# Attention weights times values in bursts of eight tiles, with the row sums behind them, and a smaller pool for weight operands

## Chip, cores and metric

The kernel runs on one core of one Trainium2 chip. The metric is the device time of one execution in microseconds (us), as the median of several runs. TensorE is called PE below, VectorE DVE, ScalarE ACT, GpSimd POOL and SyncE SP; PEld is PE's weight load, which runs beside its matmuls.

## What is computed

One layer of an encoder over 2048 tokens of width 1024, in float32. Cut to its core, the reference reads:

```python
def reference(x, ...):
    q_a, k_a, v_a, f_a, q_b, k_b, v_b = jnp.split(x @ w_in, SPLITS, axis=-1)
    y_a = forgetting_attention(q_a, k_a, v_a, log_sigmoid(f_a + b_forget))  # 8 heads, causal, FoX
    y_b = chunked_band_attention(q_b, k_b, v_b, rel_bias)                   # 8 heads, own chunk of 64 and 8 before
    x = layer_norm(ALPHA * x + concat(y_a, y_b) @ w_out)
    u = causal_conv(x @ w_up)                                               # width 3, 5632 columns
    value, gate = jnp.split(u, 2, axis=-1)
    return layer_norm(ALPHA * x + (value * gelu(gate)) @ w_down)
# in both attentions: out = softmax(q k^T / 8 + bias) v, per head of 64 columns
```

## The kernel before

Products that need float32 accuracy are made from operands split into a high and a low part (type float32r): `mm3` (lines 182 to 186) issues three matmuls, high by high, high by low and low by high. The split itself (`split`, lines 174 to 180) is one ACT copy (line 177), which makes the high part, and one DVE subtraction (line 180), which makes the low part. All of PE's big products run through `mm3`: the projections of the tokens, the output product, and both products of the feed-forward part.

**Order of the work.** The projections (`projection`) are a dense stream that is advanced a few matmuls at a time by `weave`, while `attention` (from line 498) yields once per tile of 128 keys. The attention runs twice over the heads: once with query chunks 0 and 1 (512 queries each), once with chunks 2 and 3. One unit is a head and a query chunk: 4 to 16 tiles of keys in the forgetting heads (pairs p below 4, called FoX), 4 or 8 in the band heads. What PE executes in the end is an order that a scheduler made when the program was built; it may pull instructions of one stage between those of another, and each engine runs its own list strictly in order.

**One tile.** `logits` (from line 594) makes the scores of 128 keys by up to 512 queries in a PSUM tile `st` (lines 611 and 612, two matmuls; the pool has TB = 2 buffers), adds a bias on DVE where the tile needs one (618, 621), and ACT writes the exponentials to a tile `pt` (line 623; PT = 10 buffers). `total` (629 to 632) adds each `pt` on POOL to a running tile `sums` (NSUM = 3 buffers).

**Value products.** GROUP = 4 tiles `pt` are collected; LAG_P = 4 tiles later `weigh` (693 to 698) multiplies each by its value tile `vv` into the PSUM tile `y`. A value tile has 64 columns, half of PE's array; tiles alternate between the two halves of `y`, `half = HD * (n % 2)`. These are plain float32 products, and each stands in the trace as two matmul records, while each float32r product is one.

**Row sums.** After a unit's last tile `close` joins the two halves of `y`. After the second head of a pair it defers `finish` by another LAG_S = 4 tiles. `finish` (646 to 659) sums `sums` over the 128 partitions with a product by ones (line 650, 64 columns again, one for each of the pair's heads), ACT copies the result to `row` (652; 2 buffers), DVE takes reciprocals and multiplies `yt` (656 to 658), and a DMA stores `y_d`.

**Scores' maxima.** `maxima` (from line 545) runs one unit ahead: products at line 574, maxima on DVE (577, 582). At its start SP loads `qa` and `qb` (lines 552 to 554).

**Operands for later stages.** `prepare_weights` (from line 271) is a generator, advanced once every PRE = 9 yields of the projections from yield PRE0 = 60 on. It makes 16 operands from `w_out` and 77 from `w_down` (11 blocks of 7; 55 of the 77 are a sum or difference of two tiles). It loads four raw tiles of 256 KB (`w_raw`, line 288), yields, then makes one operand per step: a DVE sum or difference (279), the split into the two halves of the one buffer `w_hl`, and one store of 512 KB (282). All DMAs are issued by SP, in order, a DMA waiting there for its buffer and its data.

Of the kernel before, what the change touches and what calls it, by code (L numbers as in the profile page):

```python
# [10 lines left out]
F32 = mybir.dt.float32  # L11
# [8 lines left out]
P = 128  # L20
# [15 lines left out]
SCALE = HD ** -0.5  # L36
NEG = -1e30
LOWEST = -3e38
PT = 10
GROUP = 4  # L40
RATE1, RATE2 = 1.1, 0.6
KV, NKB, NSUM = 5, 7, 3
DLY_E = 10
VAT = (1, 0)
VPOS = (1, 0)
WFREE = 8
LAG_P = 4
HP = 1
LAG_S = 4
LAG_R = 2  # L50
UNIT = 1.0
UNITB = 1.4
# [27 lines left out]
    ((7,), (), ((0, 1), (1, 1))),  # L80
)

PRE0, PRE = 60, 9
AHEAD_L, AHEAD_P, RESERVE = 5, 2, 16
DLY_V, DLY_R, DLY_Z = 32, 16, 16
WNEXT = 3
# [13 lines left out]
def f32(ap):  # L100
    return ap.bitcast(F32)
# [3 lines left out]
def hymba_layer(  # L105
# [165 lines left out]
    def prepare_weights(pool):  # L271

        def parts(dst, u, v=None, op=None):
            hl = tl(pool, [P, 2, CH], F32R, "w_hl")
            if v is not None:
                src = f32(hl[:, 1])
                nc.vector.tensor_tensor(src, u, v, op=op)
                u = src  # L280
            split(hl[:, 0], hl[:, 1], u, nc.scalar, nc.vector)
            nc.sync.dma_start(dst.rearrange("l p m -> p l m"), f32(hl))

        def load(src, tiles):
            raws = []
            for n, (i, j) in enumerate(tiles):
                raws.append(tl(pool, [P, CH], F32, f"w_raw{n}"))
                nc.sync.dma_start(raws[n], src[i * P : i * P + P, CH * j : CH * j + CH])
            return raws

        for k in range(0, KT, 2):
            tiles = [(k + n // 2, n % 2) for n in range(4)]
            raws = load(w_out, tiles)
            yield
            for raw, (i, j) in zip(raws, tiles):
                yield
                parts(wo_d[i, j], raw)
        HF = NF // 2
        for k in range(HF):
            raws = load(w_down, [(HF * i + k, j) for i in range(2) for j in range(2)])  # L300
            yield
            for n in DOWN:
                yield
                (k0, l0), v, op = DOWN[n][3:6]
                parts(wd_d[k, n], raws[2 * k0 + l0], v and raws[2 * v[0] + v[1]], op)


    def projection(mem, banks, state):
# [188 lines left out]
    def attention(pools, chunks, ready):  # L497
# [148 lines left out]
        def finish(p, c, sums, yt):  # L646

            ss = tl(ps_s, [P, CH], F32, "sc")
            for s in range(2):
                nc.tensor.matmul(ss[HD * s : HD * s + HD], ones, sums[s], start=True, stop=True)  # L650
            rs = tl(yp, [P, CH], F32, "row", 2)
            nc.scalar.activation(rs, ss, AF.Copy)

            def divide(t):
                part = rs[:, t * P : t * P + P]
                nc.vector.reciprocal(part, part)
                if t == TQ - 1:
                    nc.vector.tensor_mul(yt, rs, yt)
                    nc.sync.dma_start(y_d[p, :, c * CH : (c + 1) * CH], yt)

            for t in range(TQ):
                defer(LAG_R + t, lambda t=t: divide(t))
# [37 lines left out]
        def close(p, s, c, y, acc):  # L700
            if s == 0:
                yts[p, c] = tl(yp, [P, CH], F32, "yt", 3)
                sums[p, c] = acc
            join(s, c, y, yts[p, c])
            if s == 1:
                defer(LAG_S, lambda: finish(p, c, (sums[p, c], acc), yts[p, c]))

        hd, qs, ahead = start(0)
        run_all(ahead)
        for i, (p, s, c) in enumerate(work):  # L710
            nhd, nqs, ahead = start(i + 1)
            if p < 4 or c == 0:
                order = list(range(TQ * c + TQ))
            else:
                order = [TQ * c - 1, TQ * c] + list(range(TQ * c - 4, TQ * c - 1)) + list(range(TQ * c + 1, TQ * c + TQ))
            acc = tl(yp, [P, CH], F32, "sums", NSUM)
            y = tl(ps_y, [P, CH], F32, "y")
            pieces = 0
            if i + 1 < len(work):
                c1 = work[i + 1][2]  # L720
                pieces = TQ * (c1 + 1 if work[i + 1][0] < 4 else min(2, c1 + 1))
            done = 0
            tiles = []
            for n, j in enumerate(order):
                run_later(now)
                tiles.append(logits(p, s, c, hd, qs, j))
                if n:
                    total(acc, tiles[0][1] if n == 1 else None, *tiles[-1][1:])
                last = n == len(order) - 1
                if len(tiles) == GROUP:  # L730
                    defer(LAG_P, lambda y=y, t=tiles, n=n, last=last: weigh(y, t, n < GROUP, last))
                    tiles = []
                if last:
                    defer(LAG_P, lambda p=p, s=s, c=c, y=y, acc=acc: close(p, s, c, y, acc))
                while done < pieces and done * len(order) < FRAC * pieces * (n + 1):
                    next(ahead, None)
                    done += 1
                now += 1
                yield (UNIT if p < 4 else UNITB) * (UC0 if c == 0 else 1.0)
            run_all(ahead)  # L740
            hd, qs = nhd, nqs
# [652 lines left out]
```

## Time and profile before

| what | before |
|---|---|
| median of the runs | 2792.08 us (lowest 2785.5) |
| the profiled execution's own time | 2789.79 us |
| its span, first to last instruction | 2788.0 us |
| granted PE clock, mean over the span | 0.993 |
| busy: PE, DVE, ACT, POOL | 98%, 70%, 42%, 22% |

The span is what the profiler saw; 1.8 us lie around it. Busy time of PE is the time in which a matmul record is open. Matmuls overlap in the pipeline, so the cost of one is read from the distance between starts, not from its own length. Idle time before a row stands in square brackets with what ended it.

### The profile page before, as it was taken

The numbers are of one execution on the slowest core, as the hardware profiler recorded it, in microseconds if no ns is written. First come the engines' busy times: TensorE is split into PE (matmuls) and PEld (weight loads), VectorE is DVE, ScalarE is ACT, GpSimd is POOL, SyncE is SP. The second block draws the span as 40 slices with busy tenths as digits, with TensorE's granted clock in tenths as the row PEclk, the third lists the DMA queues.
The fourth block names the chain that finished last, engine by engine and source line by source line (L and its number), as shares of the span: only waits on it lengthen the run. The fifth ranks groups of instructions, "written<-read, shape, count | busy, mean of one in ns | idle before, by whom it ended". The sixth has DMA issues, their size and how long they took to land.

```text
span 2788.0 us, 38642 instructions
## 1 busy us (share of the span) xinstructions
PE 2724.5 (98%) x12632; PEld 2045.3 (73%) x12632; DVE 1941.7 (70%) x3577; ACT 1160.7 (42%) x2004; POOL 623.2 (22%) x754
## 2 busy tenths in 40 slices
PE   9999999999999999999998999999999999999998
PEld 7676767675666656766786888888887788888886
DVE  4557576777677655668568888876568877777559
ACT  4434444444444443433225555553222555544221
POOL 2235242327567555333000000000000000000000
PEclk9999999999999999999999999999999999999999
DMA  8666767665455444677894444428778222236974
GB/s 242 197 207 196 228 194 229 211 201 169 144 182 182 137 144 153 199 198 217 293 328 142 141 166 156 155 83 311 260 247 322 87 80 81 78 88 206 323 227 161
DMA packets 324618, 527.40 MB, mean 189 GB/s; under 512 B 70688, under 2 KB 86176, under 8 KB 324416
## 3 DMA queue, kind: packets, MB, share of 16 engines
q1 hardware_dynamic: 324416, 524.93, 59.1%
q8 instruction: 100, 1.64, 0.2%
q14 instruction: 102, 0.84, 0.1%
HBM read 362.65 MB, written 162.14 MB: 188 GB/s over the span
## 4 chain that ended last, share of the span: by engine, by line
PE 84%; DVE 4%; DMA 4%; ACT 1%; issue 1%; POOL 0%; SPq 0%; DVEq 0%; ACTq 0%; POOLq 0%
PE acc L184 21%; PE acc L186 21%; PE acc L185 21%; PE y L698 8%; PE st L611 4%; PE sc L574 4%; PE st L612 3%; DMA qb<-qh_d 1%; PE sc L650 1%; DVE slot L180 1%; DVE slot L1132 1%; DMA slot<-in_w_v_dram 1%; DMA wd_d<-w_hl 1%; PE acc L841 0%; DVE slot L816 0%
## 5 line engine op out<-in xcount | busy, mean ns | idle before, releaser
L184 PE MATMUL acc<-slot,slot 128*128 128x512 f32 (+2 forms) x3064 | 1165.7, 381 | 17.9 <-ACT slot L177 17.9
L186 PE MATMUL acc<-slot,slot 128*128 128x512 f32 (+2 forms) x3064 | 1160.5, 379 | 6.6 <-DVE slot L180 6.6
L185 PE MATMUL acc<-slot,slot 128*128 128x512 f32 (+2 forms) x3064 | 1161.3, 379 | 0.0
L177 ACT ACTIVATE slot<-slot 128x512 fp32r<-128x512 f32 (+1 forms) x680 | 416.4, 626 | 674.2 <-DVE slot L1121 193.0
L184 PEld LDWEIGHTS acc<-slot,slot 128*128 128x128 f32 x3064 | 580.4, 189 | 135.9 <-ACT slot L177 23.5
L186 PEld LDWEIGHTS acc<-slot,slot 128*128 128x128 f32 x3064 | 579.7, 189 | 126.2 <-DVE slot L180 10.8
L185 PEld LDWEIGHTS acc<-slot,slot 128*128 128x128 f32 x3064 | 580.4, 189 | 112.6 <-issue 2.8
L180 DVE TENSOR_TENSOR slot<-slot,slot 128x512 fp32r<-128x512 f32 (+1 forms) x652 | 450.7, 707 | 194.4 <-ACT slot L177 167.9
L632 POOL TENSOR_TENSOR sums<-sums,pt 128x512 f32<-128x512 f32 (+3 forms) x416 | 426.0, 1024 | 251.9 <-ACT pt L623 189.0
L623 ACT ACTIVATE pt<-st 128x512 f32<-128x512 f32 (+3 forms) x544 | 261.7, 492 | 333.4 <-PE st L612 121.4
L698 PE MATMUL y<-pt,vv 128*64 128x512 f32 (+3 forms) x1088 | 281.6, 505 | 0.2 <-DVE yt L640 0.2
L611 PE MATMUL st<-qa,ka 128*128 128x512 f32 (+2 forms) x544 | 209.0, 385 | 9.0 <-ACT pt L623 8.5
L574 PE MATMUL sc<-kb,qb 66*128 66x512 f32 (+2 forms) x544 | 186.6, 373 | 10.8 <-DMA qb<-qh_d 8.1
L612 PE MATMUL st<-qb,kb 97*128 97x512 f32 (+2 forms) x544 | 189.9, 357 | 4.4 <-ACT qb L592 3.9
L577 DVE TENSOR_REDUCE mx<-sc 128x1 f32<-128x512 f32 x192 | 127.9, 686 | 80.0 <-PE sc L574 78.3
L611 PEld LDWEIGHTS st<-qa,ka 128*128 128x128 f32 x544 | 103.0, 189 | 96.0 <-issue 44.1
L698 PEld LDWEIGHTS y<-pt,vv 128*64 128x64 f32 x1088 | 82.0, 136 | 124.2 <-issue 111.5
L574 PEld LDWEIGHTS sc<-kb,qb 66*128 66x128 f32 x544 | 99.5, 190 | 78.6 <-DVE mx L582 17.5
L856 DVE SCALAR_TENSOR_TENSOR v<-u,cw,v 128x1024 f32<-128x1024 f32 x88 | 113.0, 1285 | 62.4 <-ACT v L855 44.2
L1005 POOL COPY u<-halo 128x2 f32<-128x2 f32 x44 | 17.6, 401 | 620.8 <-DVE v L857 620.8
L582 DVE CUSTOM_DVE_ANT_0 junk<-sc,bq 128x512 bf16<-128x512 f32 (+2 forms) x224 | 108.2, 483 | 49.4 <-PE sc L574 40.2
L632 POOL TENSOR_TENSOR sums<-pt 128x384 f32<-128x384 f32 (+1 forms) x64 | 79.5, 1243 | 255.4 <-PE sc L650 181.4
(116 smaller groups left out, 2250.3 us busy)
## 6 DMA issues: line engine op xcount, KB each, us to landing
slot<-wd_d SPq DMA_DIRECT2D x308, 256.0 KB
slot<-in_w_up_dram SPq DMA_DIRECT2D x176, 256.0 KB
wd_d<-w_hl SPq DMA_DIRECT2D x77, 512.0 KB
slot<-wo_d SPq DMA_DIRECT2D x128, 256.0 KB
h_d<-v SPq DMA_DIRECT2D x44, 512.0 KB
slot<-h_d SPq DMA_DIRECT2D x88, 256.0 KB
slot<-in_w_qk_dram SPq DMA_DIRECT2D x66, 256.0 KB
xq_d<-slot SPq DMA_DIRECT2D x56, 256.0 KB
```

The costliest lines, as they stand in the source:

```text
L177: nc.scalar.activation(hi, src, AF.Copy)
L180: lo_eng.tensor_tensor(lo, src, f32(hi), op=ALU.subtract)
L184: nc.tensor.matmul(acc, wh, mh, start=first, stop=False, **more)
L185: nc.tensor.matmul(acc, wh, ml, start=False, stop=False, **more)
L186: nc.tensor.matmul(acc, wl, mh, start=False, stop=last, **more)
L574: nc.tensor.matmul(sc[:, m0:m1], qb[:KR, tq], kb[:KR, m0:m1], start=True, stop=True)
L577: nc.vector.tensor_reduce(m, sc[:, k0:k1], axis=AX.X, op=ALU.max)
L611: nc.tensor.matmul(st[:, w2], ka[:, js], qa[:, w2], start=True, stop=False)
L612: nc.tensor.matmul(st[:, w2], kb[:KM, js], qb[:KM, w2], start=False, stop=True)
L623: nc.scalar.activation(pt[:, w], st[:, w], AF.Exp)
L632: nc.gpsimd.tensor_tensor(acc[:, w], (acc if first is None else first)[:, w], pt[:, w], op=ALU.add)
L698: nc.tensor.matmul(y[half, w], v, pt[:, w], start=first and n < 2, stop=last and n >= len(tiles) - 2)
```

## The change

Eight tiles are collected instead of four, with LAG_P = 3; a unit's remaining tiles are taken with its last tile, so that units of 4 and 12 tiles end in a burst of four. `finish` is no longer deferred by LAG_S but called by `close` at once. There are 13 buffers `pt` instead of 10 and one buffer `row` instead of two. `prepare_weights` loads its operands one by one, a second tile `w_v` where a sum or difference is made, combines and splits in place, and stores the two parts with two DMAs of 256 KB; its pool is `w_lo` twice, `w_hi` and `w_v`. It has two steps to an operand and is advanced every PRE = 5 yields. Line numbers after it are lower by 1 to 5: line 698 becomes 693, 650 becomes 645, 623 becomes 618, 177 becomes 176.

```diff
-PT = 10
-GROUP = 4
+PT = 13
+GROUP = 8
-LAG_P = 4
+LAG_P = 3
-LAG_S = 4
-PRE0, PRE = 60, 9
+PRE0, PRE = 60, 5
...
-        def parts(dst, u, v=None, op=None):
-            hl = tl(pool, [P, 2, CH], F32R, "w_hl")
+        def rows(src, i, j):
+            return src[i * P : i * P + P, CH * j : CH * j + CH]
+
+        def operand(dst, u, v=None, op=None):
+            lo, hi = tl(pool, [P, CH], F32, "w_lo", 2), tl(pool, [P, CH], F32R, "w_hi")
+            nc.sync.dma_start(lo, u)
             if v is not None:
-                src = f32(hl[:, 1])
-                nc.vector.tensor_tensor(src, u, v, op=op)
-                u = src
-            split(hl[:, 0], hl[:, 1], u, nc.scalar, nc.vector)
-            nc.sync.dma_start(dst.rearrange("l p m -> p l m"), f32(hl))
...
+                tmp = tl(pool, [P, CH], F32, "w_v")
+                nc.sync.dma_start(tmp, v)
             yield
+            if v is not None:
+                nc.vector.tensor_tensor(lo, lo, tmp, op=op)
+            split(hi, lo, lo, nc.scalar, nc.vector)
+            nc.sync.dma_start(dst[0], f32(hi))
+            nc.sync.dma_start(dst[1], lo)
+            yield
...
-            rs = tl(yp, [P, CH], F32, "row", 2)
+            rs = tl(yp, [P, CH], F32, "row", 1)
...
             if s == 1:
-                defer(LAG_S, lambda: finish(p, c, (sums[p, c], acc), yts[p, c]))
+                finish(p, c, (sums[p, c], acc), yts[p, c])
...
-                if len(tiles) == GROUP:
+                if len(tiles) == GROUP or last:
                     defer(LAG_P, lambda y=y, t=tiles, n=n, last=last: weigh(y, t, n < GROUP, last))
```

The order of PE's list, first place: the unit of the first band head of the last pair with query chunk 1. `y<-pt,vv` is a value product, `st<-` a product for scores, `acc<-` one of the dense stream; `x2` means two in a row. Before, its eight value products stand in two bursts, with 67 other rows between them:

```order
L186 MATMUL acc<-slot_5942,slot_5237 128x264
L698 MATMUL y<-pt,vv 64x512 x2
L698 MATMUL y<-pt,vv 64x128
L698 MATMUL y<-pt,vv 64x256
L611 MATMUL st<-qa,ka 128x256
```

```order
L186 MATMUL acc<-slot_5963,slot_5255 128x264
L698 MATMUL y<-pt,vv 64x384 x2
L698 MATMUL y<-pt,vv 64x256
L698 MATMUL y<-pt,vv 64x128
L611 MATMUL st<-qa,ka 128x256
```

After the change the same unit on PE:

```order
L185 MATMUL acc<-slot_6081,slot_5360 128x264
L693 MATMUL y<-pt,vv 64x512 x2
L693 MATMUL y<-pt,vv 64x128
L693 MATMUL y<-pt,vv 64x256
L693 MATMUL y<-pt,vv 64x384 x2
L693 MATMUL y<-pt,vv 64x256
L693 MATMUL y<-pt,vv 64x128
L606 MATMUL st<-qa,ka 128x256
```

The eight have become one piece; the second burst has moved up to the first.

Second place, PE again: the row sums (`sc<-sums,ones`) of FoX pair 3 with query chunk 2. Before, they stand 24 rows behind the unit's last value product and directly ahead of the next unit's first four:

```order
L184 MATMUL acc<-slot_5224,slot_10645 128x512
L185 MATMUL acc<-slot_5225,slot_10645 128x512
L186 MATMUL acc<-slot_5224,slot_10646 128x512
L650 MATMUL sc<-sums,ones 64x512 x2
L698 MATMUL y<-pt,vv 64x512 x4
L611 MATMUL st<-qa,ka 128x512
```

After the change, from the unit's last value products on:

```order
L693 MATMUL y<-pt,vv 64x256
L693 MATMUL y<-pt,vv 64x128
L606 MATMUL st<-qa,ka 128x512
L569 MATMUL sc<-kb_966,qb_975 128x512
L569 MATMUL sc<-kb_969,qb_975 128x256
L607 MATMUL st<-qb_978,kb_954 128x512
L183 MATMUL acc<-slot_5335,slot_10909 128x512
L184 MATMUL acc<-slot_5336,slot_10909 128x512
L185 MATMUL acc<-slot_5335,slot_10910 128x512
L645 MATMUL sc<-sums,ones 64x512 x2
L606 MATMUL st<-qa,ka 128x512
```

The sums have moved up to eight rows behind the last value product, and away from the other value products.

Third place, SP's list of DMAs where the first `w_down` operands are made. Before, two stores of finished operands with the next block's four loads between them:

```order
L282 DMA wd_d<-w_hl 128x2x512
L288 DMA w_raw_3386<-in_w_down_dram 128x512
L288 DMA w_raw_3388<-in_w_down_dram 128x512
L531 DMA bq<-in_band_dram 128x640
L288 DMA w_raw_3390<-in_w_down_dram 128x512
L288 DMA w_raw_3392<-in_w_down_dram 128x512
L532 DMA bt<-in_band_t_dram 128x256
L282 DMA wd_d<-w_hl 128x2x512
```

After the change:

```order
L287 DMA wd_d<-w_hi 128x512
L288 DMA wd_d<-w_lo 128x512
L279 DMA w_lo<-in_w_down_dram 128x512
L395 DMA v_d<-slot_2190 128x4x64
L229 DMA slot_2225<-in_w_qk_dram 128x512
L229 DMA slot_2226<-in_w_qk_dram 128x512
L287 DMA wd_d<-w_hi 128x512
L288 DMA wd_d<-w_lo 128x512
L395 DMA v_d<-slot_2222 128x4x64
L279 DMA w_lo<-in_w_down_dram 128x512
L282 DMA w_v<-in_w_down_dram 128x512
```

An operand now has loads of its own; the one in the third row stands four DMAs ahead of the store of its high part.

## Rows read from the trace of the kernel before

**Rows 1.** The page: busy time by engine (part 1), the chain's shares (part 4).

```profile
PE 2724.5 (98%) x12632; PEld 2045.3 (73%) x12632; DVE 1941.7 (70%) x3577; ACT 1160.7 (42%) x2004; POOL 623.2 (22%) x754
...
PE 84%; DVE 4%; DMA 4%; ACT 1%; issue 1%; POOL 0%; SPq 0%; DVEq 0%; ACTq 0%; POOLq 0%
```

**Rows 2.** Busy us by window, both attention stages: PE, PEld, DVE, ACT, POOL, PE clock, DMA share, GB/s.

```profile
87.00:630.00 543.00, 528.34 (x2749) 378.36 (x2748) 358.39 (x890) 235.90 (x481) 185.06 (x227) 0.99 0.69 208
630.00:1340.00 710.00, 695.82 (x3313) 452.04 (x3312) 462.73 (x1067) 296.03 (x574) 376.62 (x363) 0.99 0.56 172
```

**Rows 3.** PE's timeline: start us, length us, engine, line, operation, operands, shape, count.

```profile
811.54 0.40 PE L611 MATMUL st<-qa,ka 128*128 128x512 f32 x1
811.78 0.40 PE L612 MATMUL st<-qb,kb 97*128 97x512 f32 x1
812.11 1.07 PE L698 MATMUL y<-pt,vv 128*64 128x512 f32 x2
813.11 0.73 PE L574 MATMUL sc<-kb,qb 66*128 66x512 f32 x2
813.68 0.39 PE L611 MATMUL st<-qa,ka 128*128 128x512 f32 x1
...
860.52 0.40 PE L186 MATMUL acc<-slot,slot 128*128 128x512 f32 x1
860.85 1.94 PE L698 MATMUL y<-pt,vv 128*64 128x512 f32 x8
862.72 0.39 PE L611 MATMUL st<-qa,ka 128*128 128x256 f32 x1
862.94 0.28 PE L612 MATMUL st<-qb,kb 97*128 97x256 f32 x1
863.06 0.34 PE L591 MATMUL sc<-ident_r,nm 128*1 128x128 f32 x3
```

**Rows 4.** PE's groups by line: busy us, mean ns, idle us before and its releasers.

```profile
L698 PE MATMUL y<-pt,vv 128*64 128x512 f32 (+3 forms) x1088 | 281.6, 505 | 0.2 <-DVE yt L640 0.2
L611 PE MATMUL st<-qa,ka 128*128 128x512 f32 (+2 forms) x544 | 209.0, 385 | 9.0 <-ACT pt L623 8.5 <-DVE yt L644 0.3
L574 PE MATMUL sc<-kb,qb 66*128 66x512 f32 (+2 forms) x544 | 186.6, 373 | 10.8 <-DMA qb<-qh_d 8.1 <-DVE mx L582 2.4
L650 PE MATMUL sc<-sums,ones 128*64 128x512 f32 x128 | 40.8, 618 | 3.5 <-POOL sums L632 3.5
```

**Rows 5.** Who waited for whom, POOL: us in total, times, longest us.

```profile
POOL sums L632 <- PE sc L650: 181.4, 17, 28.1
```

**Rows 6.** Exponentials (line 623), what ACT's idle time before them ended with: us, times.

```profile
  POOL sums L632: 11.6, 12
```

**Rows 7.** ACT's split copies (line 177), 87 to 1340 us: what they, then who waited.

```profile
  DMA slot<-in_w_qk_dram: 20.0, 15
  DMA slot<-in_w_v_dram: 16.4, 6
...
  PEld st L611: 6.0, 9
```

**Rows 8.** ACT's timeline ahead of a wait of PE.

```profile
1062.27 0.63 ACT L177 ACTIVATE slot<-slot 128x512 fp32r<-128x512 f32 x1 [3.36 <-DMA slot<-in_w_v_dram]
1062.80 0.58 ACT L623 ACTIVATE pt<-st 128x512 f32<-128x512 f32 x1
```

**Rows 9.** PE's timeline at three waits.

```profile
1063.43 0.39 PE L611 MATMUL st<-qa,ka 128*128 128x256 f32 x1 [2.07 <-ACT pt L623]
...
758.52 0.73 PE L574 MATMUL sc<-kb,qb 66*128 66x512 f32 x2 [2.13 <-DMA qb<-qh_d]
...
1336.47 1.56 PE L650 MATMUL sc<-sums,ones 128*64 128x512 f32 x2 [2.10 <-POOL sums L632]
```

**Rows 10.** Busy us by window behind the wait of 1063.43 us, columns as in rows 2.

```profile
1063.40:1066.80 3.40, 3.37 (x9) 1.90 (x9) 1.54 (x7) 0.77 (x2) 2.16 (x3) 0.57 0.30 91
```

**Rows 11.** SP's timeline, issue of the load that 758.52 us waited for.

```profile
752.61 0.55 SPq L554 DMA_DIRECT2D qb<-qh_d  x1
```

**Rows 12.** SP's stores of operands (line 282): issue ns min/median/max.

```profile
L282 SPq DMA_DIRECT2D wd_d<-w_hl x77: 359/377/1182, 208.5 to 1020.1; - x77
```

More of the change, by code (lines that the diff above doesn't have):

```diff
@@ L271, in prepare_weights @@
     def prepare_weights(pool):
-        def parts(dst, u, v=None, op=None):
-            hl = tl(pool, [P, 2, CH], F32R, "w_hl")
-            if v is not None:
-                src = f32(hl[:, 1])
-                nc.vector.tensor_tensor(src, u, v, op=op)
-                u = src
-            split(hl[:, 0], hl[:, 1], u, nc.scalar, nc.vector)
-            nc.sync.dma_start(dst.rearrange("l p m -> p l m"), f32(hl))
[L284 to L293, printed above, removed]
-            yield
-            for raw, (i, j) in zip(raws, tiles):
-                yield
-                parts(wo_d[i, j], raw)
+        def rows(src, i, j):
[3 more added lines that the diff above has]
+            nc.sync.dma_start(lo, u)
+            if v is not None:
+                tmp = tl(pool, [P, CH], F32, "w_v")
+                nc.sync.dma_start(tmp, v)
+            yield
+            if v is not None:
[4 more added lines that the diff above has]
+            yield
+        for k in range(KT):
+            for j in range(2):
+                yield from operand(wo_d[k, j], rows(w_out, k, j))
         HF = NF // 2
         for k in range(HF):
-            raws = load(w_down, [(HF * i + k, j) for i in range(2) for j in range(2)])
-            yield
             for n in DOWN:
-                yield
                 (k0, l0), v, op = DOWN[n][3:6]
-                parts(wd_d[k, n], raws[2 * k0 + l0], v and raws[2 * v[0] + v[1]], op)
+                yield from operand(
+                    wd_d[k, n], rows(w_down, HF * k0 + k, l0), v and rows(w_down, HF * v[0] + k, v[1]), op
+                )
     def projection(mem, banks, state):
```

## Prediction

> **What bounds the kernel now.** I read the page's busy line and its chain first. PE is busy 98% of the span, 84% of the chain that ended last is PE, and no other engine has over 4% of it [rows 1]. So time goes only where PE's own list gets shorter, or where PE waits. Next I read the windows of the two attention stages, because nearly all of the change lies there: PE is busy 528.34 of 543 us and 695.82 of 710 us, so 14.7 + 14.2 = 28.9 us of idle is all that shorter waits can give back in 1253 us, while DVE stands at 66% and 65% and the DMA engines at 69% and 56% [rows 2]. Then I read PE's timeline for what value products cost by their neighbours [rows 3], the groups by line for what PE waits for [rows 4], and last the waits of POOL, ACT and SP, since those engines feed PE [rows 5 to 12].
>
> **What a group of value products costs.** Busy time cannot tell this, since matmuls overlap; I take distances between starts. Between neighbours of the usual kind a matmul of 512 columns takes 0.235 us (811.54 to 811.78) and one of 256 takes 0.12 us (862.94 to 863.06) [rows 3]. One value tile by itself: from 811.78 to 813.68 are 1.90 us, less three matmuls of 0.235 us (the one ahead, and the two L574 behind), is 1.20 us. Four tiles in one piece: from 860.52 to 862.94 are 2.42 us, less 0.235 and 0.12, is 2.07 us [rows 3]. Four tiles cost 0.87 us more than one. This fits two tiles side by side in the two halves of the array: one is one pass, four are two passes, a pass of 512 columns takes 0.87 us and the entry and exit of the group 1.20 - 0.87 = 0.33 us. A tile without a partner pays a whole pass. Narrow tiles take their share of a pass. The sums (L650) have the same 64 columns and are counted alike; their mean of 618 ns a record stands near the value products' 505 [rows 4].
>
> **Part 1, the bursts.** I count groups (value products and sums that stand together without another matmul between) over the whole list of PE in both programs. Before there are 236, and 302.3 passes when partners are laid side by side; by the prices above 236 x 0.33 + 302.3 x 0.87 = 340.9 us. The two records' busy time, 281.6 + 40.8 = 322.4 us, lies close to it [rows 4]. After the change there are 218 groups and 289.5 passes: 71.9 + 251.9 = 323.8 us. That is 17.1 us less, 5.9 from 18 fewer entries and 11.1 from partners found. It is far less than eight in place of four suggests, for two reasons that the order shows. The scheduler still breaks bursts: only 20 groups hold eight value products, and 72 value tiles stand alone (91 before). And the sums lose their company: groups that hold sums beside value products fall from 28 to 6, and groups of sums alone rise from 6, 7.2 us, to 28, 28 x 1.20 = 33.6 us. All other matmuls are the same in number and shape. PE is on the path here, so I take -17 in full.
>
> **Part 2, sums right behind.** POOL's first addition of a unit waits for a `sums` buffer, which only the product by ones frees: 181.4 us in 17 waits, up to 28.1 [rows 5]. This makes POOL late, and through full `pt` buffers it held exponentials 12 times for 11.6 us [rows 6]. Finishing about five tiles earlier and three more `pt` remove most of that. PE gains at most what it waited for exponentials, 8.5 us [rows 4], and at least nothing, since most of these waits have another cause (rows 8, below). I take -2. Against it, the sums may now ask for POOL's last addition too early; PE has waited 3.5 us for that [rows 4] and I leave this as it is, because POOL no longer starts late. If it does, this is rival B. One `row` buffer instead of two: ACT's next copy comes a unit later, at least eight tiles, and the division is done five tiles after the copy; nothing, and if late, a wait of ACT ahead of exponentials, as in part 3. LAG_P = 3: a unit's last exponentials have a tile's time less. PE has waited on no `pt` here (0.2 us on something else [rows 4]); nothing.
>
> **Part 3, operands made one by one.** The splits, DVE's sums and their number stay (93 and 55). DMAs rise from 60 loads and 93 stores to 148 loads and 186 stores, 181 more; at 0.38 us an issue [rows 12] that is 69 us of SP's time in about 950, and 88 x 0.26 = 23 MB more, about 24 GB/s beside 208 and 172 [rows 2], so neither SP nor the DMA engines become the limit. What counts is lateness. ACT takes its list in order, so a split that waits for its load holds the exponentials behind it. Before, this happened at 1062.27 us: ACT waited 3.36 us for a load, the exponential behind it started at 1062.80, and PE's scores waited 2.07 us for its buffer [rows 8, 9]. The next 3.4 us ran at a granted clock of 0.57 of full, that is mostly at 1.2 GHz instead of 2.4, some 1.7 us more [rows 10].
>
> How long does a load take? The `qb` load issued at 752.61 us released PE at 758.52, 5.9 us later [rows 9, 11]. The new loads are asked for one step ahead, five yields or 15 matmuls of the dense stream, with attention between: 950 us over some 930 yields make 5.1 us. So some will be late by a little.
> The Trainium skill's page "DMA: Bandwidth & Descriptors", section "Anatomy of one DMA", fits, for DMAs that GpSimd issues, a fixed cost of about 2.0 us plus its bytes at 436 GB/s; by that rule 256 KB would land in an estimated 2.6 us and no load would be late. The row above took more than twice that, so I go by the row.
>
> The nearest rows for the count are the `in_w_qk` loads, also asked for ahead: 15 waits among 66 loads in this window, 1.3 us each [rows 7]. At that rate 93 operands give 21 waits. The present splits, with 15 + 6 waits on two kinds of loads and more on others, made PE's scores wait 9 times, 6.0 us in all [rows 7]. As many again is the upper end, +6.0 and a few stretches at half clock; the lower end is nothing, since the waits on the old one-buffer store go. I take half, 3.0, and one stretch of 1.7: +5. A second new wait is on SP: 26 of the 91 loads that reuse a `w_lo` buffer stand at most five DMAs behind the store that frees it, and hold what is behind them, `qb` loads among others. PE has waited 8.1 us for `qb` [rows 4]. This is inside the +5 at low, rival A at high.
>
> **Sum.** -17 - 2 + 5 = -14 against the profiled execution's own 2789.8 us, which lies 2.3 us below the median of the runs: 2776. About 2%, 56 us, is what a measurement of this kernel can tell from no change, so this is a small gain inside it.
>
> **Rivals.**
> A, slower: late operand loads. Place: ACT's splits ahead of exponentials, and SP's loads behind a buffer wait. If one in ten of the 93 loads costs PE what the load at 1062 us cost, 9 x (2.07 + 1.7) = 34 us, the time is 2790 - 17 - 2 + 34 = 2805. It decides from five such events on (19 us, all that the bursts and POOL's part give). For it: the 5.1 us lead against 5.9 us of flight. Against: of the 21 waits on two kinds of loads and all others, only nine reached PE.
> B: the sums wait for POOL. Place: the product by ones, now eight rows behind the last value product where it was 24. At 1336 us PE waited 2.10 us there [rows 9]. If eight of the 32 do, with half clock behind each, 8 x 3.8 = 30, and 2790 - 17 + 30 = 2803. Against: POOL was late mostly because `sums` buffers came late [rows 5].
> C: idle goes too. Thirteen `pt` and an earlier POOL loosen the coupling, and half of the 28.9 us of idle [rows 2] goes, with half of the clock's 1% of 1253 us, 6 us: 2790 - 17 - 14 - 6 = 2753.
> D: the change doesn't do what it says. The saved PE time comes back as waits, because ACT, DVE and loads keep their pace: 2790. Against: DVE at 66% [rows 2].
>
> **Chances.** The forecast (2765 to 2788) 0.58, C 0.13, D 0.09, A 0.13, B 0.07. The range takes in C and A: 2753 to 2805. Only C with much more could pass 2% to the fast side (2736 against the median), only A with twice its events to the slow side (2848): 0.02 and 0.03.
>
> **What would show it.** Right: value products and sums together lose some 17 us by starts, sums alone cost 1.20 each, POOL's wait for the product by ones falls from 181 us to well under 100, and exponentials stop waiting for POOL. Part 3 shows as new waits of ACT for `w_lo` loads, some 20 of them, with PE's waits for exponentials between 6 and 15 us. The forecast is wrong if those exceed 25 us, if PE's wait for `sums` passes 10 us, or if the idle time in the two windows falls under 15 us.

## The result, and the profile after

The change makes the kernel slower. Before ran at 2788.79 us in this comparison (median; lowest 2782.03), after at 2828.98 us (lowest 2823.43): ratio 1.0145, 95% interval 1.0127 to 1.0164, some 40 us. The ratio is of fast runs alone and so leaves out one of the four runs of before, which took 12486.5 us and is still in the median. The result lies within the 2% band and outside the predicted range. The profiled execution after has a span of 2824.8 us and a mean granted clock of 0.985 (before 2788.0 and 0.993 [rows 1]).

The page after, busy time by engine and the chain's shares, as in [rows 1]:

```profile
PE 2734.6 (97%) x12632; PEld 2052.6 (73%) x12632; DVE 1939.6 (69%) x3577; ACT 1159.7 (41%) x2004; POOL 625.3 (22%) x754
...
PE 55%; DVE 3%; DMA 2%; ACT 1%; issue 0%; SPq 0%; DVEq 0%; ACTq 0%
```

As a share of the span, no engine has become busier. The chain could be followed back over only some 61% of the span, 55% of it on PE, so it says little about the first stages; the two attention stages are read from their windows. After, same columns as [rows 2]:

```profile
87.00:630.00 543.00, 507.28 (x2578) 355.00 (x2577) 335.16 (x822) 222.88 (x458) 180.87 (x220) 0.96 0.73 216
630.00:1340.00 710.00, 692.46 (x3334) 460.17 (x3333) 455.81 (x1073) 294.48 (x570) 369.14 (x356) 0.98 0.62 190
```

PE is idle 35.7 + 17.5 = 53.3 us where it was 28.9; the clock lost three points in the first window; and the DMA engines' share rose from 0.69 and 0.56 to 0.73 and 0.62. PE's groups after, as in [rows 4] (the fourth was idle for 0.0 before):

```profile
L693 PE MATMUL y<-pt,vv 128*64 128x512 f32 (+3 forms) x1088 | 265.5, 509 | 0.1
L606 PE MATMUL st<-qa,ka 128*128 128x512 f32 (+2 forms) x544 | 205.1, 381 | 17.1 <-ACT pt L618 8.8 <-DMA qa<-qh_d 8.0
L569 PE MATMUL sc<-kb,qb 66*128 66x512 f32 (+2 forms) x544 | 196.2, 391 | 15.9 <-DMA qb<-qh_d 5.3 <-DVE mx L572 4.8 <-DVE mx L577 2.6
L586 PE MATMUL sc<-ident_r,nm 128*1 128x128 f32 x256 | 26.9, 228 | 10.7 <-DVE nm L583 10.7
L645 PE MATMUL sc<-sums,ones 128*64 128x512 f32 x128 | 41.0, 660 | 0.0
```

The value products are shorter by 16 us, as forecast, and PE does not wait for the row sums at all. Waits for exponentials stand where they stood (8.8 against 8.5). New are waits for loads of `qa` (8.0) and for the negated maxima `nm` (10.7).

To see all of PE's time I cut the list of its matmuls into distances from start to start, and each distance into the idle part that the timeline gives, the part lost to a granted clock below 1 (length of such a stretch times one minus its clock), and the rest, apart for the matmuls with 64 columns (value products and sums). In us; the 13 to 14 us that a row lacks to its span lie ahead of the first matmul's start and behind the last one's:

| kernel | idle | lost to the clock | 64-column matmuls | all others | span |
|---|---|---|---|---|---|
| before | 50.2 | 16.2 | 296.0 | 2411.9 | 2788.0 |
| after | 76.7 | 35.5 | 280.7 | 2418.0 | 2824.8 |
| after, old operand pool (below) | 54.9 | 18.1 | 283.5 | 2412.2 | 2782.0 |
| before, new operand pool (below) | 72.3 | 33.6 | 300.1 | 2423.1 | 2842.5 |

The bursts give 15.3 us. Idle time costs 26.5 more, the clock 19.3 and slower neighbours 6.1.

Where is it? I took the time at which a given unit's last value product ends. Against before, after is 13 us behind at the 16th of 64 units (352.1 and 365.2 us), 50 us behind at the 32nd (611.6 and 661.3), and 40 behind at the 64th (1333.5 and 1373.1). So the heaviest loss lies in the eight units after 495 us, where the second half's tokens are loaded. SP's list there, after (start, length, line, DMA):

```profile
486.62 0.32 SPq L287 DMA_DIRECT2D wd_d<-w_hi  x1
487.35 0.32 SPq L288 DMA_DIRECT2D wd_d<-w_lo  x1
487.76 11.04 SPq L314 DMA_DIRECT2D slot<-in_xT_dram  x13
...
502.22 0.60 SPq L548 DMA_DIRECT2D qa<-qh_d  x1
...
528.92 0.42 SPq L229 DMA_DIRECT2D slot<-in_w_qk_dram  x1
```

The 11.04 us of the thirteen token loads are not all issuing: each issue took 0.33 to 0.84 us, and in between SP waited, longest for a split that freed a buffer (us in total, times, longest):

```profile
SPq L314 <- DVE slot L179: 3.7, 1, 3.7
```

And PE's timeline behind it (idle time ahead of a row in brackets):

```profile
505.42 0.39 PE L185 MATMUL acc<-slot,slot 128*128 128x512 f32 x1
508.34 0.47 PE L606 MATMUL st<-qa,ka 128*128 128x512 f32 x1 [2.53 <-DMA qa<-qh_d]
...
511.99 1.58 PE L569 MATMUL sc<-kb,qb 66*128 66x384 f32 x2
517.27 0.59 PE L586 MATMUL sc<-ident_r,nm 128*1 128x128 f32 x4 [3.69 <-DVE nm L583]
...
534.18 0.41 PE L569 MATMUL sc<-kb,qb 66*128 66x256 f32 x1
534.39 0.63 PE L183 MATMUL acc<-slot,slot 128*128 128x512 f32 x1
```

Read it from the end. For 29 us, from 505.42 to 534.39, PE's list has no product of the dense stream. It isn't the tokens that are missing there: ACT had copied the last of them by 503.80 us,

```profile
503.17 0.63 ACT L176 ACTIVATE slot<-slot 128x512 fp32r<-128x512 f32 x1 [0.29 <-DMA slot<-in_xT_dram]
```

and DVE had subtracted it by 504.61. PE's list, which the build made, goes on with attention here, and the next weights of the dense stream were loaded only at 528.92. Attention alone has to fill PE, and its own chain is late: `qa` was issued behind thirteen token loads, `nm` is 3.69 us late. The window of that stretch and, for comparison, 500 to 550 us before and after:

```profile
508.80:539.50 30.70, 24.87 (x62) 11.75 (x61) 19.73 (x56) 8.74 (x18) 11.34 (x17) 0.50 0.66 193
500.00:550.00 50.00, 41.33 (x132) 22.00 (x131) 32.17 (x82) 15.57 (x32) 17.14 (x26) 0.69 0.70 193
```

```profile
500.00:550.00 50.00, 49.13 (x239) 33.76 (x238) 37.18 (x103) 22.97 (x52) 24.84 (x35) 1.00 0.72 217
```

For 30.7 us the granted clock is 0.50, the lower of the two levels (1.2 of 2.4 GHz). DVE's timeline tells why `nm` was late:

```profile
513.20 1.76 DVE L651 RECIPROCAL row<-row 128x128 f32<-128x128 f32 x2
514.88 0.63 DVE L577 CUSTOM_DVE_ANT_0 junk<-sc,bq 128x512 bf16<-128x512 f32 x1
515.43 0.08 DVE L577 DVE_READ_ACCUMULATOR2_ANT mx<- 128x1 f32 x1
515.43 1.76 DVE L651 RECIPROCAL row<-row 128x128 f32<-128x128 f32 x2
517.11 0.10 DVE L583 TENSOR_REDUCE nm<-mx 128x4 fp32r<-128x4 f32 x1
```

The reciprocals of a pair's row sums, which the change moved up, stand 3.5 us long ahead of the maxima. POOL's wait for the product by ones fell less than I said, from 181.4 [rows 5]:

```profile
POOL sums L627 <- PE sc L645: 130.2, 12, 37.1
```

What ended ACT's idle time before exponentials, as in [rows 6]:

```profile
  POOL sums L627: 10.9, 14
```

And ACT's waits in front of operand splits, 87 to 1340 us (us in total, times, longest): the sum on DVE or the load itself was late 36 times, 68 us in all.

```profile
ACT w_hi L176 <- DVE w_lo L285: 53.3, 29, 6.4
ACT w_hi L176 <- DMA w_lo<-in_w_down_dram: 15.0, 7, 3.4
```

### The profile page after: what moved, and what is told of

Its sections match the earlier page's. It is cut to its first block, busy times and chain, and to the rows that moved or that the text cites. A ratio compares the mean times of both kernels' runs of the same rounds, so it can differ in the third digit from the quotient of the medians.

```text
span 2824.8 us, 38838 instructions
## 1 busy us (share of the span) xinstructions
PE 2734.6 (97%) x12632; PEld 2052.6 (73%) x12632; DVE 1939.6 (69%) x3577; ACT 1159.7 (41%) x2004; POOL 625.3 (22%) x754
## 4 chain that ended last, share of the span: by engine, by line
PE 55%; DVE 3%; DMA 2%; ACT 1%; issue 0%; SPq 0%; DVEq 0%; ACTq 0%
PE acc L185 17%; PE acc L184 17%; PE acc L183 17%; PE y L693 2%; PE sc L569 1%; PE st L606 1%; PE st L607 1%; DVE slot L1127 1%; DVE slot L811 1%; DVE slot L179 1%; PE acc L836 0%; DMA slot<-in_w_qk_dram 0%; DVE slot L1144 0%; DMA slot<-y_d 0%; DMA slot<-wo_d 0%
## 5 line engine op out<-in xcount | busy, mean ns | idle before, releaser
L693 PE MATMUL y<-pt,vv 128*64 128x512 f32 (+3 forms) x1088 | 265.5, 509 | 0.1
L569 PE MATMUL sc<-kb,qb 66*128 66x512 f32 (+2 forms) x544 | 196.2, 391 | 15.9 <-DMA qb<-qh_d 5.3
```

What stands on the lines that cost most here:

```text
L569: nc.tensor.matmul(sc[:, m0:m1], qb[:KR, tq], kb[:KR, m0:m1], start=True, stop=True)
L693: nc.tensor.matmul(y[half, w], v, pt[:, w], start=first and n < 2, stop=last and n >= len(tiles) - 2)
```

## The experiments

All times are compared with before on the same chip (its medians there 2786.4 to 2790.2 us); a ratio of 0.001 is 2.8 us.

| run | median us | ratio, 95% interval |
|---|---|---|
| 1 before, new operand pool | 2842.56 | 1.0200, 1.0176 to 1.0224 |
| 2 after, old operand pool | 2779.74 | 0.9970, 0.9958 to 0.9981 |
| 3 before, sums at once | 2804.17 | 1.0059, 1.0039 to 1.0078 |
| 4 after, PRE 6 | 2799.39 | 1.0050, 1.0030 to 1.0071 |
| 5 as 2, sums deferred | 2775.38 | 0.9960, 0.9949 to 0.9970 |
| 6 after, no operand steps near the token loads | 2820.20 | 1.0115, 1.0085 to 1.0145 |
| 7 after, stores a step later | 2827.50 | 1.0146, 1.0117 to 1.0176 |
| 8 after, sums deferred | 2823.26 | 1.0135, 1.0115 to 1.0155 |
| 9 after, PRE 8 | 2818.88 | 1.0107, 1.0091 to 1.0124 |
| 10 as 2, one more load an operand | 2802.15 | 1.0049, 1.0032 to 1.0066 |
| 11 after, loads a step ahead | 2814.20 | 1.0087, 1.0069 to 1.0106 |
| 12 after, RATE1 1.2 | 2822.06 | 1.0136, 1.0118 to 1.0154 |
| 13 before, RATE1 1.0 | 2843.42 | 1.0215, 1.0195 to 1.0236 |
| 14 as 4, sums deferred | 2793.39 | 1.0029, 1.0016 to 1.0042 |
| 15 after, no sums or splits of operands | 2809.59 | 1.0074, 1.0059 to 1.0089 |
| 16 after, no loads of operands | 2770.40 | 0.9931, 0.9914 to 0.9948 |
| 17 after, operand loads by POOL | 2879.84 | 1.0336, 1.0308 to 1.0364 |
| 18 after, operand loads by ACT | 2828.40 | 1.0147, 1.0125 to 1.0169 |

Runs 3, 4, 5, 9, 10, 11, 14 and 15 came out between the forecasts that were made for them, runs 16 and 17 outside all of theirs (16 faster, 17 slower).

**Which part of the change?** Run 1 puts only the new `prepare_weights` and PRE 5 into the kernel before; run 2 takes only these out of the change; run 3 only calls `finish` at once in the kernel before.

```diff
 run 1, against before
-PRE0, PRE = 60, 9
+PRE0, PRE = 60, 5
...
 run 2, against after
-PRE0, PRE = 60, 5
+PRE0, PRE = 60, 9
-PT = 13
+PT = 11
...
 run 3, against before
-                defer(LAG_S, lambda: finish(p, c, (sums[p, c], acc), yts[p, c]))
+                finish(p, c, (sums[p, c], acc), yts[p, c])
```

> The kernel before with the new operand pool and its rate alone (one operand at a time, own loads, two stores, every fifth yield). Theory S (the operands' DMAs keep SP from loading the second half's tokens, PE's dense stream runs out near 500 us): 2820 to 2845 us, about 50 above before, with over 30 us of idle and half clock between 450 and 700 us. Theory F (the sums right behind bring the reciprocals ahead of the maxima) and theory B (bursts of eight set attention and dense stream out of step): 2785 to 2800 us.

> The change with the old operand pool and its rate, which leaves room for 11 tiles of weights. Theory S: 2765 to 2782 us, the forecast gain of the bursts without the loss. Theories F and B: 2805 to 2835 us, the loss stays.

> The kernel before with the row sums right behind alone. Theory F: 2805 to 2835 us, PE waits for the negated maxima over 8 us in all. Theories S and B: 2783 to 2800 us.

The pool alone costs 56 us (the whole of it idle time, clock and neighbours, as the table by starts shows); without it the change gains 8. Sums at once cost 16 by themselves; by starts neither idle time nor the clock shows it (49.5 and 17.6), the other matmuls stand 8 us wider, and I did not find out why.

**How fast are the operands made, and are the sums too early?**

> The change with an operand step every sixth yield instead of every fifth, 13 operands then left for the end of the projections. Theory S, if what counts is which operand DMAs fall on the reload of the tokens: 2765 to 2795 us and no stretch without dense matmuls near 510 us. Theories F and B: 2815 to 2835 us as in the change.

> Bursts of eight with the old operand pool and its rate, 11 tiles of weights, and the row sums deferred by four tiles again, as before. If the bursts and the sums right behind add (bursts worth some 17 us, sums at once costing 11 to 18 as in the run with them alone): 2764 to 2774 us, faster than both kernels. If the bursts gain only the 7 us of the run with both: 2776 to 2786 us.

> The change with the row sums deferred by four tiles again and nothing else. If the sums at once cost the change what they cost the kernel before: 2808 to 2820 us, PE's wait for negated maxima under 5 us instead of 10.7. If their cost is hidden behind the late operands: 2822 to 2835 us.

```diff
 run 4, against after
-PRE0, PRE = 60, 5
+PRE0, PRE = 60, 6
...
 runs 5, 8 and 14, against runs 2, after and 4
-                finish(p, c, (sums[p, c], acc), yts[p, c])
+                defer(4, lambda: finish(p, c, (sums[p, c], acc), yts[p, c]))
```

One step less in six gives back 27 us. Its windows have PE at nearly its old busy time in the first stage, with the DMA share back at 0.69:

```profile
87.00:630.00 543.00, 526.01 (x2736) 374.87 (x2734) 348.65 (x868) 231.89 (x473) 188.05 (x227) 0.99 0.69 215
```

Deferring the sums again gives 3 to 6 us wherever bursts are (runs 5, 8, 14). Run 5 beats both kernels by about 11 and 52 us.

**Is it the place, or SP's waits for splits?**

> The change, but no operand step from yield 480 to 559 of the projections, where the second half's tokens are loaded; afterwards every fourth yield, so that all operands are made. Theory S1 (the loss comes from operand DMAs that meet the reload of the tokens): 2775 to 2800 us, the first pass's last eight units under 130 us instead of 166. Theory S2 (it comes from the number of DMAs and their bytes anywhere): 2820 to 2840 us.

> The change with each operand's two stores issued one step later, with two w_hi buffers and 12 tiles of weights, so that SP seldom waits for ACT's split. If SP's waits for the splits are what holds the tokens' loads: 2780 to 2805 us and SP's waits of w_hi stores for ACT under 10 us where the change has 24 between 400 and 700 us. If it is the operand DMAs' place and number ahead of the tokens' loads: 2815 to 2840 us.

```diff
 run 6, against after
-                if n >= PRE0 and n % PRE == 0:
+                if PRE0 <= n < 480 and n % PRE == 0 or n >= 560 and n % 4 == 0:
...
 run 7, against after (w_hi has two buffers, PT = 12)
             split(hi, lo, lo, nc.scalar, nc.vector)
+            yield
             nc.sync.dma_start(dst[0], f32(hi))
             nc.sync.dma_start(dst[1], lo)
-            yield
```

Run 6 empties the place of the largest loss, and the place recovers: from 500 to 650 us idle time and clock cost 12 us in place of 38. But only some 8 us of the total come back, because the other stretches, now at a step every fourth yield, pay instead. In run 7 SP's wait for the high part, 200 to 700 us, halves, and the time does not move. SP after, then run 7:

```profile
SPq L287 <- ACT w_hi L176: 37.2, 27, 4.1
```

```profile
SPq L288 <- ACT w_hi L176: 18.9, 15, 5.0
```

So it is neither the place nor that wait.

**Late landings, or the amount of traffic?**

> The changed kernel with PRE = 8 in place of 5: a step of the operands every eighth dense yield, so all their DMAs, splits and buffers stay as they are and come more thinly. Late landings (the operands' loads have not landed when, one step later, their split stands in the queues of ScalarE and VectorE): at PRE 5 a step comes about every 6 us in the stretch 200 to 700 us (84 stores in 500 us), at PRE 8 about every 9.5 us, so the loads have landed; ScalarE's wait for late operands (37.2 and 12.6 us in the stretch 87 to 800 us) falls under 30 us together and the time is 2775 to 2792 us, near the kernel with the old pool (2780). Amount (each DMA of the operands costs the stage a share, by how many there are in a stretch): 3/8 fewer steps give back 3/8 of the 47 us between the old and the new pool, 2806 to 2812. Neither: 2820 or more.

> The kernel with the bursts and the old operand pool (the one that ran at ratio 0.997), with one more load of 256 KB for each of the 112 operands of w_down, into a tile of its own that nothing reads, and PT 10 in place of 11 to make room for it. In the stretch 200 to 700 us that is some 45 loads more, about as many as the new pool has (74 for 24). Nothing waits for them but the next of them. Late landings: nothing comes late, 2778 to 2790 (ratio up to 1.001). Amount: the extra loads are what costs, 2805 to 2825 (ratio 1.007 to 1.014).

> The changed kernel, PRE 5 as it stands, with each operand's loads issued before the split of the operand ahead of it, so that three steps lie between a load and its split in place of one; w_lo gets three buffers and w_v two, and PT falls from 13 to 11. The same loads, stores, splits and bytes, at the same rate. Late landings: ScalarE's and VectorE's waits for operands in the stretch 87 to 800 us (37.2, 12.6 and 15.7 us) fall to under half and most of the 47 us come back, 2780 to 2797. Amount: 2820 to 2830. Order (the program's order on TensorE has a stretch of dense products alone and then one of attention alone behind the reload of the tokens, and it has it here too): 2815 to 2830 with the half clock at 490 to 540 us still there, and ScalarE's waits for operands gone.

```diff
 run 10, against run 2 (PT = 10)
+                extra = tl(pool, [P, CH], F32, "w_x")
+                nc.sync.dma_start(extra, w_down[(HF * k0 + k) * P : (HF * k0 + k) * P + P, CH * l0 : CH * l0 + CH])
                 parts(wd_d[k, n], raws[2 * k0 + l0], v and raws[2 * v[0] + v[1]], op)
...
 run 11, against after (w_lo has three buffers, w_v two, PT = 11)
+        for job in jobs:
+            following = operand(*job)
+            yield
+            if rest:
+                rest()
+            yield
+            rest = following
```

Each theory gets a part. In run 10 the operands of `w_down` are 77, not the 112 of the text, so 77 loads that nothing reads cost 2802.15 - 2779.74 = 22 us, 0.29 us each. No engine that computes waits for their data, but SP does: they share one buffer, and SP's list stood 24 times until the load before had landed, with attention's loads behind it (87 to 1340 us):

```profile
SPq L305 <- DMA w_x<-in_w_down_dram: 47.3, 24, 4.1
```

So the 0.29 us are a price of a load with its wait in SP's list, not of its bytes alone. (PT is 10 here and 11 in run 2; ACT's waits ahead of exponentials that value products or POOL ended are the same, 8.8 and 8.4 us.) The DMA share of its first stage is that of the change, 0.73 (0.68 in run 2):

```profile
87.00:630.00 543.00, 520.82 (x2670) 368.32 (x2671) 346.65 (x862) 231.29 (x475) 184.48 (x227) 0.97 0.73 218
```

In run 11 all loads stay and come earlier against their splits; 16 us come back (1.0145 to 1.0087). Whether ACT's and DVE's waits fell as the expectation asked is not shown, and PT is 11 there in place of 13. Run 9 missed both forecasts, and its windows from 87 to 800 and 800 to 1345 us, then those of after, show why:

```profile
87.00:800.00 713.00, 690.65 (x3495) 477.21 (x3494) 448.16 (x1060) 302.95 (x607) 286.60 (x313) 0.99 0.64 198
800.00:1345.00 545.00, 513.72 (x2444) 341.82 (x2443) 354.50 (x855) 220.59 (x429) 260.52 (x266) 0.97 0.68 208
```

```profile
87.00:800.00 713.00, 670.99 (x3293) 460.31 (x3291) 448.88 (x1048) 293.03 (x587) 269.00 (x295) 0.95 0.70 209
800.00:1345.00 545.00, 533.74 (x2640) 358.98 (x2640) 347.08 (x855) 226.95 (x445) 281.01 (x282) 1.00 0.62 190
```

At PRE 8 the first stretch gains 20 us of busy PE, and the second loses 20: the operands are not done when the projections end, and line 1257 makes the rest in one go. By the 40th unit run 9 is 38 us ahead of after (854.8 and 893.0 us), by the 64th 4.

**Is it the stretches without dense products?** The build orders PE's list anew for every kernel, and the kernels that lost most have such stretches behind the token loads. RATE1 sets how much of the dense stream goes with a unit.

```diff
 run 12, against after
-RATE1, RATE2 = 1.1, 0.6
+RATE1, RATE2 = 1.2, 0.6
...
 run 13, against before
-RATE1, RATE2 = 1.1, 0.6
+RATE1, RATE2 = 1.0, 0.6
```

> The changed kernel with RATE1 = 1.2 in place of 1.1: in the first pass over the heads a unit of attention takes 9% more of the dense stream with it; operands, their DMAs and PRE stay. In the program's order of TensorE no stretch of the first pass's second half lacks dense products for long behind the reload of the tokens (two shorter ones stand later). Dense-free stretches (the loss arises where TensorE's list has attention alone for over 10 us, because there it waits for attention's own chain and the clock falls to half): 2785 to 2808, with at most 25 us of idle time and half clock in such stretches, where the changed kernel has 45. Traffic (the operands' DMAs cost wherever they run): 2820 to 2832.

> The kernel before with RATE1 = 1.0 in place of 1.1: no part of the change, the old operand pool and its traffic; in the first pass a unit of attention takes 9% less of the dense stream. TensorE's order then has some 140 us of stretches without dense products for over 10 us, where before has 43. Dense-free stretches: 2815 to 2850, with over 35 us of idle time and half clock in these stretches, where before has 1. Traffic: within 10 us of before, as no DMA is added.

> The changed kernel with PRE = 6 and the row sums deferred by 4 tiles as before: bursts, 13 tiles of weights and the new operand pool kept. Its order has two dense-free stretches (12.8 and 14.5 us of TensorE's time). Dense-free stretches: 2775 to 2790 (the same with the sums at once ran at 2799, and deferring them gave 4 us with the old pool). Traffic: 2795 to 2805.

In the trace, before has 43 us of dense-free stretches of over 10 us with 1 us of idle time and clock loss in them, after 87 us with 40 (45 in the expectations, which count the half clock in the idle time as well). Run 12 did not do what it was for: its trace still has 91 us of them, with 30 us lost. Run 13 decides. Its time, 55 us above before without one DMA more, is what the theory forecast and rules out traffic as the only thing that can cost so much: another order alone can. But its sign is missing, and as the cause of the change's loss the theory falls: run 13 has fourteen such stretches, 235 us in all, and loses only 19 us in them, 11 of these in one, at 608 us, where PE waits for splits of projection weights. Its own loss lies elsewhere: by starts the 64-column matmuls take 29 us more than before and the others 18, while after lost idle time and clock. One stretch of it, 23 us without a dense product, with no idle time and a full clock:

```profile
668.00:691.00 23.00, 23.00 (x86) 10.71 (x85) 10.54 (x25) 11.62 (x22) 19.98 (x16) 1.00 0.45 144
```

The DMA share there is 0.45, in the bad stretch of after 0.66. Here attention alone fills PE, with its chain on time. Run 14 came out between its two forecasts.

**Which half of an operand?** Run 15 leaves out the sums and the splits of the operands and stores the loaded tiles as they are; run 16 leaves out their 148 loads and makes every operand from one tile. Both give later stages other numbers.

```diff
 run 15, against after
-            if v is not None:
-                nc.vector.tensor_tensor(lo, lo, tmp, op=op)
-            split(hi, lo, lo, nc.scalar, nc.vector)
-            nc.sync.dma_start(dst[0], f32(hi))
+            nc.sync.dma_start(dst[0], lo if v is None else tmp)
...
 run 16, against after
-            nc.sync.dma_start(lo, u)
-            if v is not None:
-                tmp = tl(pool, [P, CH], F32, "w_v")
-                nc.sync.dma_start(tmp, v)
...
+        raw = tl(pool, [P, CH], F32, "w_v")
+        nc.sync.dma_start(raw, rows(w_out, 0, 0))
```

> The changed kernel, all the operands' loads and stores and PRE 5 kept, but nothing made of them: the sums on VectorE, the copies on ScalarE and the subtractions on VectorE are left out, and the stores send the loaded tiles as they are, so later stages work on other numbers. ScalarE and VectorE have nothing of the operands in their queues that could hold the exponentials and maxima. Held queues (late operands stop ScalarE and VectorE in front of attention's own work): 2775 to 2795. DMAs (the loads and stores themselves, on SyncE's list and the DMA engines, make attention's own loads late): 2812 to 2830.

> The changed kernel with every sum, split and store of the operands and PRE 5 kept, but their 148 loads left out: all operands are made from one tile that is loaded once, so later stages work on other numbers. Held queues: nothing comes late any more except the stores that free w_hi, 2775 to 2795. DMAs: 148 of the 334 operand DMAs are gone; if the loads cost, 2775 to 2800, if the stores do, 2812 or more. Together with the run without splits: both low means held queues, this one low and the other high means the loads, both high the stores.

Run 16 is the clearest of all: without the loads the loss is gone, and the rest of the change, with PRE 5, all splits and all stores, is 19 us faster than before. It lacks more than the change added, for the kernel before has 60 such loads. Its first stage has PE busy for 528.87 us and a DMA share of 0.65:

```profile
87.00:630.00 543.00, 528.87 (x2747) 376.71 (x2748) 374.16 (x900) 240.22 (x490) 192.16 (x232) 0.99 0.65 201
```

Run 15, with nothing of the operands on ACT and DVE, lies between its two forecasts: it gets back 20 us and keeps 21. What PE waits for there (us in total, times, longest), over both stages:

```profile
PE sc L566 <- DMA qb<-qh_d: 10.1, 12, 3.2
PE sc L583 <- DVE nm L580: 9.4, 6, 3.7
...
PE st L603 <- DMA qa<-qh_d: 4.6, 3, 2.8
```

The loads of `qb` and `qa` cost 14.7 us, and in run 16 these are

```profile
PE sc L569 <- DMA qb<-qh_d: 4.2, 7, 0.9
```

alone; before waited 8.1 us for `qb` and not at all for `qa` [rows 4]. So attention's own loads come late beside the operands' loads, even when neither ACT nor DVE waits for an operand. SP still waits for them in run 15: its two stores now stand directly behind the loads' landing (87 to 1340 us).

```profile
SPq L285 <- DMA w_lo<-in_w_down_dram: 30.5, 28, 3.2
SPq L284 <- DMA w_v<-in_w_down_dram: 29.3, 28, 2.9
```

**By SP's list, or by the bytes?** Both runs leave nothing out; another engine issues the loads.

```diff
 run 17 (run 18: nc.scalar), against after
-            nc.sync.dma_start(lo, u)
+            nc.gpsimd.dma_start(lo, u)
...
-                nc.sync.dma_start(tmp, v)
+                nc.gpsimd.dma_start(tmp, v)
```

> The changed kernel, nothing left out and PRE 5, with the operands' 148 loads issued by GpSimd instead of SyncE: the same bytes from and to the same places, in a list of another engine. SyncE's list (the loads and what they wait for stand ahead of attention's and the tokens' loads, and set the order there): 2770 to 2790, faster than the kernel before or level with it. DMA engines (the bytes in flight slow the other loads): 2812 to 2830. If GpSimd's issues cost its additions of the row sums, exponentials wait for GpSimd over 10 us and the time lies between, 2790 to 2812.

> The same with the 148 loads issued by ScalarE: 148 issues of about 0.4 us are 59 us of ScalarE, busy 41% of the span, in front of exponentials. SyncE's list: 2772 to 2795. DMA engines: 2812 to 2830. A load that waits for its buffer holds the exponentials behind it; if that decides, over 2800 with TensorE's waits for exponentials (8.8 us in the changed kernel) over 20 us.

Taking the loads off SP's list gives nothing back. That speaks for the bytes, but not cleanly, for the loads bring waits of their own to the new list. POOL's in run 17, ahead of its additions, and DVE's in run 18:

```profile
POOL w_v L282 <- DVE w_lo L285: 90.1, 27, 5.8
...
POOL w_lo L279 <- DMA wd_d<-w_lo: 44.3, 17, 8.4
```

```profile
DVE w_lo L285 <- DMA w_lo<-in_w_down_dram: 40.7, 16, 7.1
```

The Trainium skill's page "DMA: Bandwidth & Descriptors", section "Issuing engines are not separate DMA queues", says that DMAs started by different engines run on the same DMA engines and that spreading them saves only the time of issuing. Run 18 agrees (1.0147 beside 1.0145); in run 17 the waits above hide what it would show.

The bytes alone are not shown to be the cause either. Taken from the issue to the last update of its semaphore, the median load of `qa` between 87 and 630 us was under way for 3.04 us before, 3.27 after, 3.07 in run 16, 3.33 in run 18 and 3.69 in run 15; one of `qb` for 3.68, 3.77, 3.32, 3.92 and 3.71. After, two of the three loads of `qa` that PE waited for were under way for 3.52 and 3.13 us, no longer than usual, and were late because SP had issued them late.

## Why the prediction was wrong

**Part 1 (bursts, -17) was right in what it priced.** By starts the 64-column matmuls cost 296.0 - 280.7 = 15.3 us less, and 12.5 less in run 2. As time less of it arrives: run 2, with parts 1 and 2 and without part 3, gains 8 us of the forecast 19, because idle time and clock take 6.6 back.

**Part 2 (sums right behind, -2) failed in its means, at little cost.** POOL's wait stayed at 130 us, where I had said well under 100, and exponentials wait for POOL as before. What I priced at nothing was DVE: the reciprocals now stand ahead of the next unit's maxima. Deferring the sums again is worth 3 to 6 us with bursts; without them the step costs 16.

**Part 3 (operands one by one, +5) is the step that failed.** It cost 49 us between runs 2 and after (1.0145 - 0.9970) and 56 in run 1. I wrote that "neither SP nor the DMA engines become the limit", from averages: 69 us of issuing in 950, and 24 GB/s more. Averages hid it. I put the loads themselves at nothing and priced only splits that come late; but run 16 loses nothing, and run 10, with 77 loads that nothing reads, loses 22 us. By these runs two prices can be estimated in place of the +5. The loads, with their waits in SP's list: 88 more at the 0.29 us of run 10 are 26 us. The late operands in front of ACT and DVE: 20 us by run 15, 16 by run 11. Together 42 to 46; that they add up is argued, not shown. My own sum without part 3's loads was 2790 - 17 - 2 = 2771, and run 16 ran at 2770.4, but that is luck: it also lacks the 60 loads of before, and run 2, which has them, ran at 2779.74.

A reading behind the +5 was wrong too: the 66 `in_w_qk` loads are those of the whole span, and 56 are issued between 87 and 1340 us. The rate then gives 25 late splits instead of 21; ACT had 36, for 68 us.

Rival A had the second price, at 34 us, and nothing of the first: it looked in the right places, ACT's splits and SP's buffer waits, but counted late operands, not loads as such. PE's waits for exponentials, which I had set as the sign, hardly moved (8.8 us, inside my 6 to 15), while `qa`, `nm` and the half clock behind them took the loss. Rival B did not happen (0.0 us), and neither did C or D.

What stays open: by which path the loads cost PE time, in SP's list, in the DMA engines or both (the times under way and run 10's waits speak for SP's list; run 18, where ACT issues the loads and no time comes back, speaks against SP's list alone); and how much of it works through PE's order, which the build changes with every added load and which alone was worth 55 us in run 13.

## What to carry to other kernels

Price an added transfer in the stage where it runs, and in the list that issues it, not against an average of the span; here a load that nothing reads cost 0.29 us. Count what a smaller pool adds: four shared loads became twelve here, and with the loads left out the loss was gone. Background work can have a best rate: here a step every sixth yield was better than every fifth, and every eighth left a heap at the end that cost most of what it had won (38 us ahead at the 40th unit, 4 at the 64th).

## What the runs showed of the hardware

- Thirteen token loads of 256 KB in a row held SP for 11.04 us, though one issue took 0.33 to 0.84 us, 0.43 in the median: SP's list stands at every buffer that is not free, here once for 3.7 us.
- With a DMA share of 0.73 in place of 0.69 in the first stage, the median load of `qa` was under way for 3.27 us instead of 3.04, and the median load of tokens for 4.70 instead of 4.07.
- PE stayed at half clock for 30.7 us although it was busy for 24.87 of them; the gaps ahead of it and in it were of up to 3.7 us. With no gaps, 23 us of the same kind of work ran at full clock.
- Loads issued by POOL in place of SP cost 53 us more (1.0336 and 1.0145), with POOL waiting 90.1 and 44.3 us for them and their buffers ahead of its additions; issued by ACT they cost the same as by SP (1.0147).
